# A fixed engine order for the query, key and value projections of a hybrid encoder layer

## The chip, the cores and the metric

One NeuronCore of a Trainium2 chip runs the whole layer in one launch. The metric is device time in microseconds, the median of the runs of the kernel. PE is the tensor engine (matrix products and transposes by product), DVE the vector engine, ACT the scalar engine, POOL the gpsimd engine, SP the queue from which this kernel issues its DMAs, also the transposing ones.

## The reference, cut to what matters

The layer normalizes x (1024 tokens by 1024), projects it to everything that its three branches need, and adds the gated branches' sum back to x. The part around the change makes queries, keys and values of eight heads from small latents:

```
q = (rmsnorm(q_lat, q_norm_g) @ w_uq).reshape(B, S, 8, 96)
kv = (rmsnorm(kv_lat, kv_norm_g) @ w_ukv).reshape(B, S, 8, 64 + 64)
k_nope, v = split_cols(kv, (64, 64))
k = concatenate([k_nope, k_rope], axis=-1)      # k_rope: 32 columns, the same for all heads
q = rope_tail(rmsnorm(q, q_head_g), cos, sin)
k = rope_tail(rmsnorm(k, k_head_g), cos, sin)
```

The gates (silu of 512 columns for each of two branches, sigmoids of 3 x 1024) are products of the normalized x with other columns of the same input weight. All is float32; each product is made as three, from the high and low parts of both sides.

## The kernel before, in words

Phase 1 normalizes x, turned with features in partitions (tiles hh and hl, high and low part), and makes the latents of eight blocks of 128 tokens. Then comes the loop of this case, one step for each block t:

- stD(t) (line 322) rotates the shared key columns (rope_k's four DVE operations, lines 327 to 330), makes the value product on PE (6 matmuls of 512 columns, line 333), which ACT and DVE read out as high and low part (line 335, through evac, lines 95 and 96) and SP stores; then the key product (6 matmuls, line 340), its squares on ACT (343), their sums on DVE (345), the power -1/2 on POOL (105) and the multiplications on DVE (348, 349); then the queries in two groups of four heads (9 matmuls of 384 columns each, line 359) with the same norm (362 to 367), and their rotation on POOL (370 to 374).
- stC(t + 1) (line 311) turns the next block's latents by PE into tile tr, and ACT and DVE read them out as high and low part (lath, latl).
- stE(t) (line 376) copies the 16-bit halves of keys and queries into pl (two DVE copies each, line 381), and SP issues two transposing DMAs each (line 382) into plt. Keys and queries share the one buffer of plt.
- stF(t - 1) (line 384) puts the turned halves together again on ACT (four reads of plt for keys, four for queries, line 391, into pw), scales them on ACT into the high part (line 98) and on DVE into the low part (line 99) of qkt, which SP stores (line 395). Each of keys and queries is done in two groups of four heads. An edge (issue_after) keeps it behind the last query square of step t.

PE is filled with dense products of the gate columns (class method feat, lines 518 to 535; tile fm while this loop runs, mm later): a generator yields one matmul of 512 columns at a time, and pull(n) asks for n of them. An item is 128 feature columns, 48 matmuls in two halves of 24. A half's result is read out by ACT (line 603) and DVE (604). The weights of the next item are split into high and low part on POOL (lines 74 and 80, tiles whi and wlo), in one piece where self.parts is 1, in quarters at the third, 11th, 19th and 27th matmul of the running item where it is 4; behind the last quarter SP is asked for the item after. The loop pulls 9 at five places of each step from t = 3 on, none for t = 0 to 2, and 60 behind the loop. What comes next, phase 2, goes on pulling from the same generator.

The order of the instructions on each engine is not the order of the code: a scheduler lays the queues out when the program is built, by priority in the order of the code and by when it expects an operand to be ready. manual_schedule(engines=...) keeps the order of the code on the engines it lists; phase 1 has it for PE (closed before this loop) and the attention stages later have it too. Engines wait for one another by semaphores that the framework sets.

PSUM has eight banks: in this loop tr takes two, the projections (mm) three, the dense products (fm) three. lath, latl, pw and qkt have two buffers each; plt, kn, qn, sq and vst have one.

Of the kernel before, what the change touches and what calls it, by code (L numbers as in the profile page):

```python
# [62 lines left out]
class K:  # L63
# [161 lines left out]
    def phase1(self, sr):  # L225
        tc, nc, a, d = self.tc, self.nc, self.a, self.d
        v, gp = nc.vector, nc.gpsimd
        with ExitStack() as st:
# [93 lines left out]
            def stD(tb, pulls):  # L322
                hi, lo = LT.pop(tb)
                _, kro, spe = HN.pop(tb)
# [6 lines left out]
                pv = ps.tile([P, 4, 2, DV], F32, name="mm", bufs=3)  # L331
                for k in range(2):
                    self.mm3(pv, hi[:, 3 + k, :], lo[:, 3 + k, :], wkh[:, k, 512:], wkl[:, k, 512:], k == 0, k == 1)
                vst = wd.tile([P, 4, 4, DV], F32R, name="vst")
                self.evac(pv, vst[:, :, 0:4:3, :], vst[:, :, 1:3, :])
                nc.sync.dma_start(d["v"][:, tb].rearrange("p h c -> p (h c)"), vst.rearrange("p a b c -> p (a b c)").bitcast(F32))
                self.pull(pulls)
                pk = ps.tile([P, H, DN], F32, name="mm", bufs=3)
                for k in range(2):
                    self.mm3(pk, hi[:, 3 + k, :], lo[:, 3 + k, :], wkh[:, k, :512], wkl[:, k, :512], k == 0, k == 1)  # L340
                kn = KN[tb] = wd.tile([P, H, DH], F32, name="kn")
# [4 lines left out]
                v.tensor_scalar_add(s[:, :H], s[:, :H], spe)  # L346
                self.rstd(s[:, H:], s[:, :H], DH)
                v.tensor_tensor(out=kn[:, :, :DN], in0=pk, in1=s[:, H:].unsqueeze(2).broadcast_to([P, H, DN]), op=ALU.mult)
                v.tensor_tensor(out=kn[:, :, DN:], in0=kro[:, 3, :].unsqueeze(1).broadcast_to([P, H, DR]),
                                 in1=s[:, H:].unsqueeze(2).broadcast_to([P, H, DR]), op=ALU.mult)  # L350
                self.pull(pulls)
                qn = QN[tb] = wd.tile([P, H, DH], F32, name="qn")
                s = wd.tile([P, 2 * H], F32, name="qst", bufs=2)
                pqs = []
                for g in range(2):
                    pq = ps.tile([P, 4, DH], F32, name="mm", bufs=3)
                    pqs.append(pq)
                    for k in range(3):
                        self.mm3(pq, hi[:, k, :], lo[:, k, :], wqh[:, k, g * 384:(g + 1) * 384], wql[:, k, g * 384:(g + 1) * 384], k == 0, k == 2)
                    hs = slice(4 * g, 4 * g + 4)  # L360
                    sq = wd.tile([P, H, DN], F32, name="sq").rearrange("p a b -> p (a b)")[:, :4 * DH].rearrange("p (a b) -> p a b", b=DH)
                    self.last = nc.scalar.activation(out=sq, in_=pq, func=AF.Square).ins
                    rs = slice(H + 4 * g, H + 4 * g + 4)
                    v.tensor_reduce(out=s[:, hs], in_=sq, axis=AX.X, op=ALU.add)
                    self.rstd(s[:, rs], s[:, hs], DH)
                    self.pull(pulls)
                    v.tensor_tensor(out=qn[:, hs, :], in0=pq, in1=s[:, rs].unsqueeze(2).broadcast_to([P, 4, DH]), op=ALU.mult)
# [8 lines left out]
            def stE(tb):  # L376
                for N, n in ((KN, "k"), (QN, "q")):
                    src, pl = N[tb], self.pl[n]
                    t = N[tb] = wd.tile([P, 2, H, P], U16, name="plt", bufs=1)
                    for x in range(2):  # L380
                        v.tensor_copy(pl[:, x, :, :DH], _halves(src, x))
                        nc.sync.dma_start_transpose(t[:, x], pl[:, x].rearrange("p a b -> p (a b)"))

            def stF(tb):
                ts = slice(tb * P, (tb + 1) * P)
                for src, dst, i in ((KN.pop(tb), d["k"], 1), (QN.pop(tb), d["q"], 0)):
                    for g in range(2):
                        hs = slice(4 * g, 4 * g + 4)
                        w = wd.tile([DH, 4, P], F32, name="pw", bufs=2)
                        for x in range(2):  # L390
                            nc.scalar.copy(_halves(w, x), src[:DH, x, hs])  # L391
                        t = wd.tile([DH, 4, 2, P], F32R, name="qkt", bufs=2)
                        self.evac(w, t[:, :, 0, :], t[:, :, 1, :], self.hg[:, i:i + 1])
                        for x in range(2):
                            nc.sync.dma_start(dst[4 * g:4 * g + 4, :, x, ts].rearrange("h d s -> d h s"), t[:, :, x, :].bitcast(F32))
# [64 lines left out]
            self.mm = lambda hf: ps.tile([P, 512], F32, name="fm", bufs=3)  # L460
# [4 lines left out]
            for t in range(TB):  # L465
                pulls = 9 if t > 2 else 0
                stD(t, pulls)
                if t + 1 < TB:
                    stC(t + 1)
                self.pull(pulls)  # L470
# [759 lines left out]
```

## Time and profile before

| | |
|---|---|
| median of 3 runs | 1171.45 us (1171.41 to 1172.24) |
| the profiled execution | 1175.43 us |
| its span, first to last instruction | 1173.3 us |
| mean granted TensorE clock | 0.986 |
| busy in the span: PE, DVE, POOL, ACT | 96%, 61%, 49%, 47% |
| matmuls | 5458 |

A profile is one execution, recorded by the chip. Times in it count from the start of the span. A matmul's duration in it is modelled and overlaps the next one's, so how fast PE works is read from the distance of starts. In the views, an arrow (kst <- sq) means that the first tile is made from the second; a wait names the waiting instruction first and what released it behind the arrow. The lines are those of the kernel before; a line can be that of a helper (evac, rstd, split), which several places call.

### The profile page before, as it was taken

How to read it: one execution, taken by the hardware profiler on the slowest of the kernel's cores; microseconds unless marked ns; L12 is line 12 of the kernel's file. 1: busy time of each engine (PE TensorE's matmuls, PEld its weight loads, DVE VectorE, ACT ScalarE, POOL GpSimd, SP SyncE). 2: the span in 40 equal slices, each digit the busy share in tenths (PEclk: the TensorE clock that was granted, in tenths of full speed). 3: DMA queues.
4: the chain of work that ended last, by engine and by line, in shares of the span. 5: the costliest groups of instructions: out<-in, count | busy, mean ns of one | idle time of the engine just before them, and what ended most of it. 6: DMA issues, size and time to landing. Idle time of an engine off the chain costs nothing.

```text
span 1173.3 us, 15384 instructions
## 1 busy us (share of the span) xinstructions
PE 1131.3 (96%) x5458; PEld 949.7 (81%) x5458; DVE 713.0 (61%) x1077; ACT 548.3 (47%) x821; POOL 576.7 (49%) x520
## 2 busy tenths in 40 slices
PE   7999899899999999998989999999999999999998
PEld 7998787778888888887868877878778878888887
DVE  6997686243335433454269999999999205655221
ACT  6446575511011114656358878878778312322100
POOL 4455475243324553345655777776785823333200
PEclk8999999999999999999989999999999989999999
DMA  8427999923232333455889989999997597545341
GB/s 300 150 94 185 240 232 238 261 101 107 73 124 73 126 108 81 90 144 158 243 209 208 220 215 213 211 229 236 213 198 167 162 408 291 160 140 169 105 148 50
DMA packets 284717, 207.75 MB, mean 177 GB/s; under 512 B 201664, under 2 KB 253504, under 8 KB 284544
## 3 DMA queue, kind: packets, MB, share of 16 engines
q1 hardware_dynamic: 284640, 206.76, 65.7%
q8 instruction: 43, 0.70, 0.2%
q14 instruction: 34, 0.28, 0.1%
HBM read 108.14 MB, written 50.33 MB: 135 GB/s over the span
## 4 chain that ended last, share of the span: by engine, by line
PE 27%; DVE 14%; DMA 6%; issue 4%; POOL 2%; ACT 1%; SPq 0%; ACTq 0%; DVEq 0%; POOLq 0%
DVE pl L85 6%; DVE mx L989 4%; PE mm L714 4%; PE mm L716 4%; PE mm L712 4%; DMA plt<-pl 3%; DVE ptl L1014 3%; PE mm L111 2%; PE mm L109 2%; PE mm L110 2%; PE mm L527 2%; PE mm L529 2%; PE mm L531 2%; PE po L1028 1%; PE s L984 1%
## 5 line engine op out<-in xcount | busy, mean ns | idle before, releaser
L527 PE MATMUL mm<-hh,whi 128*128 128x512 f32 x672 | 265.0, 394 | 3.5 <-DVE sg L604 3.5
L529 PE MATMUL mm<-hl,whi 128*128 128x512 f32 x672 | 264.4, 393 | 0.0
L531 PE MATMUL mm<-hh,wlo 128*128 128x512 f32 x672 | 262.9, 393 | 1.2 <-POOL wlo L80 1.2
L74 POOL TENSOR_SCALAR whi<-wraw 128x256 fp32r<-128x256 f32 (+1 forms) x128 | 117.2, 916 | 201.1 <-PE pm L761 76.4
L90 ACT COPY pw<-plt 128x1024 uint16<-128x1024 uint16 (+1 forms) x160 | 197.8, 1302 | 6.8 <-DMA plt<-pl 6.5
L80 POOL TENSOR_TENSOR wlo<-wraw,whi 128x256 fp32r<-128x256 f32 (+1 forms) x129 | 178.4, 1383 | 11.2 <-ACT whi L76 1.4
L527 PEld LDWEIGHTS mm<-hh,whi 128*128 128x128 f32 x672 | 127.5, 190 | 30.5 <-DVE sg L604 4.3
L531 PEld LDWEIGHTS mm<-hh,wlo 128*128 128x128 f32 x672 | 127.5, 190 | 28.3 <-POOL wlo L80 1.6
L529 PEld LDWEIGHTS mm<-hl,whi 128*128 128x128 f32 x672 | 127.6, 190 | 26.0
L85 DVE COPY pl<-p 128x1024 uint16<-128x1024 uint16 x144 | 127.7, 927 | 17.1 <-DMA plt<-pl 9.3
L1010 POOL TENSOR_SCALAR pth<-pw 128x1024 fp32r<-128x1024 f32 x64 | 78.6, 1228 | 91.5 <-ACT pw L90 87.7
L984 PE MATMUL s<-k,q 96*128 96x512 f32 x384 | 101.1, 399 | 6.1 <-ACT p L992 5.9
L1014 DVE TENSOR_TENSOR ptl<-pw,pth 128x1024 fp32r<-128x1024 f32 x64 | 98.8, 1543 | 6.8 <-POOL pth L1010 6.4
L992 ACT ACTIVATE p<-s,mx 128x1024 f32<-128x1024 f32 x64 | 71.5, 1117 | 60.9 <-DVE mx L989 60.2
L984 PEld LDWEIGHTS s<-k,q 96*128 96x128 f32 x384 | 72.2, 190 | 25.7 <-ACT p L992 9.6
L989 DVE TENSOR_REDUCE mx<-s 128x1 f32<-128x1024 f32 x64 | 77.2, 1206 | 5.8 <-PE s L984 5.4
L689 ACT ACTIVATE sg<-sg 128x1024 f32<-128x1024 f32 x24 | 25.5, 1061 | 92.6 <-DMA sg<-d_r 92.6
L391 ACT COPY pw<-plt 96x512 uint16<-96x512 uint16 x64 | 43.8, 771 | 27.1 <-DMA plt<-plq 20.9
L621 ACT ACTIVATE sg<-mm,small 128x512 f32<-128x512 f32 x48 | 32.7, 683 | 46.5 <-PE mm L531 34.2
L719 DVE TENSOR_TENSOR acc<-mm,sg 128x512 f32<-128x512 f32 x16 | 10.9, 689 | 53.0 <-PE mm L716 42.6
L76 ACT CAST whi<-wraw 128x1024 fp32r<-128x1024 f32 x9 | 9.5, 1051 | 68.1 <-PE mm L529 66.8
L1028 PE MATMUL po<-pth,v 128*128 128x256 f32 x256 | 38.4, 293 | 0.0
(323 smaller groups left out, 2331.3 us busy)
## 6 DMA issues: line engine op xcount, KB each, us to landing
wraw<-in_w_feat SPq DMA_DIRECT2D x48, 512.0 KB, 4.1
d_r<-sg SPq DMA_DIRECT2D x24, 512.0 KB, 3.4
sg<-d_r SPq DMA_DIRECT2D x24, 512.0 KB, 4.2
d_k<-qkt SPq DMA_DIRECT2D x32, 192.0 KB, 3.0
d_q<-qkt SPq DMA_DIRECT2D x32, 192.0 KB, 2.9
q<-d_q SPq DMA_DIRECT2D x32, 192.0 KB, 3.6
wraw<-in_w_br SPq DMA_DIRECT2D x12, 512.0 KB, 4.2
k<-d_k SPq DMA_DIRECT2D x14, 384.0 KB, 5.1
```

What stands on the lines that cost most here:

```text
L74: nc.gpsimd.tensor_scalar(out=hi, in0=raw, scalar1=1.0, scalar2=1.0, op0=ALU.mult, op1=ALU.mult)
L80: e.tensor_tensor(out=lo, in0=raw, in1=hi.bitcast(F32), op=ALU.subtract)
L85: self.nc.vector.tensor_copy(pl[:, x], _halves(src, x))
L90: self.nc.scalar.copy(_halves(out, x), plt[:, x])
L527: mm(o, w1, self.hh[:, k, c], start=k == 0, stop=False)
L529: mm(o, w1, self.hl[:, k, c], start=False, stop=False)
L531: mm(o, w2, self.hh[:, k, c], start=False, stop=k == KT - 1)
L984: nc.tensor.matmul(s[:, c], q[:, qi, ts], k[:, ki, c], start=s_, stop=e_)
L989: v.reduce_max(out=mx[:, 1:2], in_=s, axis=AX.X, negate=True)
L992: nc.scalar.activation(out=p, in_=s, func=AF.Exp, bias=mx[:, 1:2], accum_out=mx[:, 2:3])
L1010: nc.gpsimd.tensor_scalar(out=parts(i)[0], in0=p, scalar1=1.0, scalar2=1.0, op0=ALU.mult, op1=ALU.mult)
L1014: v.tensor_tensor(out=lo, in0=PW.pop(i), in1=hi.bitcast(F32), op=ALU.subtract)
```

## The change

The functions stD, stE and stF are taken apart into values, rope_k, keys, keys2, queries, queries2, rope_q, turn and parts, with the same operations. The loop calls them in a fixed order under manual_schedule for PE, DVE, ACT and POOL; SP's queue is still laid out by the scheduler. The projections get four banks instead of three, the dense products two instead of three. The pulls are 9 at five places for steps 3 to 7, as before, 30 in a ninth step and 30 behind the loop. The splits of the weights go in quarters inside the loop.

```
-                pv = ps.tile([P, 4, 2, DV], F32, name="mm", bufs=3)
+            mm_ps = lambda sh: ps.tile(sh, F32, name="mm", bufs=4)
...
-            def stE(tb):
-                for N, n in ((KN, "k"), (QN, "q")):
-                    src, pl = N[tb], self.pl[n]
-                    t = N[tb] = wd.tile([P, 2, H, P], U16, name="plt", bufs=1)
+            def turn(tb, N, n):
+                src, pl = N[tb], self.pl[n]
+                t = N[tb] = wd.tile([P, 2, H, P], U16, name="plt", bufs=1)
+                for x in range(2):
+                    v.tensor_copy(pl[:, x, :, :DH], _halves(src, x))
+                    nc.sync.dma_start_transpose(t[:, x], pl[:, x].rearrange("p a b -> p (a b)"))
+
+            def parts(tb, N, n, i):
+                ts = slice(tb * P, (tb + 1) * P)
+                src, dst = N.pop(tb), d[n]
+                for g in range(2):
+                    hs = slice(4 * g, 4 * g + 4)
+                    w = wd.tile([DH, 4, P], F32, name="pw", bufs=2)
                     for x in range(2):
...
+                        nc.scalar.copy(_halves(w, x), src[:DH, x, hs])
+                    t = wd.tile([DH, 4, 2, P], F32R, name="qkt", bufs=2)
+                    self.evac(w, t[:, :, 0, :], t[:, :, 1, :], self.hg[:, i:i + 1])
+                    for x in range(2):
+                        nc.sync.dma_start(dst[4 * g:4 * g + 4, :, x, ts].rearrange("h d s -> d h s"), t[:, :, x, :].bitcast(F32))
...
-            self.mm = lambda hf: ps.tile([P, 512], F32, name="fm", bufs=3)
+            self.mm = lambda hf: ps.tile([P, 512], F32, name="fm", bufs=2)
...
-            for t in range(TB):
-                pulls = 9 if t > 2 else 0
-                stD(t, pulls)
-                if t + 1 < TB:
-                    stC(t + 1)
-                self.pull(pulls)
-                stE(t)
+            E = mybir.EngineType
+            man = st.enter_context(ExitStack())
+            man.enter_context(tc.manual_schedule(engines={E.PE, E.DVE, E.Activation, E.Pool}))
+            self.parts = 4
+            for t in range(TB + 1):
+                n = 9 if 2 < t < TB else 0
+                if t < TB:
+                    rope_k(t)
+                    values(t)
+                    self.pull(n)
+                    if t + 1 < TB:
+                        stC(t + 1)
                 if t:
-                    with tc.issue_after(self.last):
-                        stF(t - 1)
-            stF(TB - 1)
-            self.pull(60)
+                    parts(t - 1, KN, "k", 1)
+                    turn(t - 1, QN, "q")
+                if t < TB:
+                    keys(t)
+                    self.pull(n)
+                    queries(t, 0)
+                    keys2(t)
+                    self.pull(n)
+                    queries(t, 1)
+                    queries2(t, 0)
+                    self.pull(n)
+                else:
+                    self.pull(30)
+                if t:
+                    parts(t - 1, QN, "q", 0)
+                if t < TB:
+                    turn(t, KN, "k")
+                    queries2(t, 1)
+                    rope_q(t)
+                    self.pull(n)
+            man.close()
+            self.parts = 1
+            self.pull(30)
```

keys ends with the power of the norm and keys2 multiplies by it; queries and queries2 share the work of a group in the same way.

## Rows read from the trace of the kernel before

**Rows 1.** The page's first part: busy us, share of the span, instructions.

```profile
PE 1131.3 (96%) x5458; PEld 949.7 (81%) x5458; DVE 713.0 (61%) x1077; ACT 548.3 (47%) x821; POOL 576.7 (49%) x520
```

**Rows 2.** Stretches: length, busy PE, PEld, DVE, ACT, POOL, granted clock, DMA, GB/s.

```profile
74.20:116.20 42.00, 41.92 (x209) 35.91 (x208) 33.31 (x81) 24.31 (x49) 27.80 (x25) 1.00 0.68 174
116.20:201.20 85.00, 78.43 (x357) 65.59 (x357) 62.95 (x116) 56.08 (x97) 47.16 (x43) 0.98 1.00 240
```

**Rows 3.** Waits from 76 to 206 us: total us, times, longest us.

```profile
ACT pw L391 <- DMA plt<-plq: 19.0, 7, 5.5
...
DVE vst L96 <- ACT vst L95: 9.6, 4, 4.5
...
PE mm L109 <- DVE vst L96: 6.6, 4, 2.3
```

**Rows 4.** Timeline of SP's queue, transposes alone: start, us, instruction.

```profile
88.79 2.72 SPq L382 DMA_TRANSPOSE plt<-plk  x2
...
100.35 2.61 SPq L382 DMA_TRANSPOSE plt<-plq  x2
...
107.03 4.96 SPq L382 DMA_TRANSPOSE plt<-plk  x2
...
157.86 4.34 SPq L382 DMA_TRANSPOSE plt<-plk  x2
...
208.10 2.62 SPq L382 DMA_TRANSPOSE plt<-plk  x2
```

**Rows 5.** Timeline of ACT around one handover.

```profile
150.60 1.33 ACT L98 ACTIVATE qkt<-pw,small 96x512 fp32r<-96x512 f32 x2
...
155.80 2.03 ACT L391 COPY pw<-plt 96x512 uint16<-96x512 uint16 x3
```

**Rows 6.** Groups by form, 74 to 201.2 us: busy us, mean ns, idle before.

```profile
L527 PE MATMUL fm<-hh,whi 128*128 128x512 f32 x96 | 38.1, 397 | 0.0
...
L99 DVE SCALAR_TENSOR_TENSOR qkt<-pw,small,qkt 96x512 fp32r<-96x512 f32 x25 | 20.8, 839 | 7.0 <-ACT qkt L98 7.0
...
L381 DVE COPY plk<-kn 128x768 uint16<-128x768 uint16 x16 | 10.8, 714 | 0.0
```

**Rows 7.** Timeline of PE; in brackets the idle time before and its releaser.

```profile
111.83 0.39 PE L527 MATMUL fm<-hh,whi 128*128 128x512 f32 x1
...
115.00 0.39 PE L531 MATMUL fm<-hh,wlo 128*128 128x512 f32 x1
...
191.57 0.45 PE L109 MATMUL mm<-wuqh,lath 128*128 128x384 f32 x1 [2.27 <-DVE vst L96]
...
200.98 0.39 PE L531 MATMUL fm<-hh,wlo 128*128 128x512 f32 x1
...
209.30 0.73 PE L527 MATMUL mm<-hh,whi 128*128 128x512 f32 x1 [2.49 <-DVE sg L604]
```

**Rows 8.** The first stretch, instructions on fm alone: busy PE, PEld, DVE, ACT.

```profile
74.20:116.20 42.00, 23.30 (x92) 16.93 (x92) 1.35 (x2) 1.67 (x3) 1.00 0.68 174
```

**Rows 9.** POOL: one query rotation, then quarters of a split, 560 to 800 us.

```profile
90.17 0.47 POOL L370 TENSOR_TENSOR sq<-qn,tabs 128x128 f32<-128x128 f32 x1 [1.37 <-DVE qn L367]
...
91.96 0.74 POOL L374 TENSOR_TENSOR qn<-qn,sq 128x256 f32<-128x256 f32 x1
...
L80 POOL TENSOR_TENSOR wlo<-wraw,whi 128x256 fp32r<-128x256 f32 x44 | 42.0, 955 | 3.5
L74 POOL TENSOR_SCALAR whi<-wraw 128x256 fp32r<-128x256 f32 x44 | 38.2, 869 | 10.3 <-DMA wraw<-in_w_feat 9.0 <-PE mm L529 1.2
```

**Rows 10.** Timeline of DVE in step 0.

```profile
85.55 2.28 DVE L349 TENSOR_TENSOR kn<-kro,kst 128x256 f32<-128x256 f32 x1
```

**Rows 11.** Stretches behind two of PE's waits, columns as in rows 2.

```profile
192.00:195.00 3.00, 3.00 (x12) 2.80 (x11) 2.48 (x6) 1.12 (x2) 0.00 (x0) 0.56 1.10 213
195.00:198.00 3.00, 3.00 (x13) 2.43 (x12) 1.93 (x6) 2.27 (x5) 2.49 (x2) 0.88 1.01 259
...
209.00:212.00 3.00, 2.70 (x7) 2.15 (x8) 2.51 (x5) 1.36 (x3) 0.00 (x0) 0.57 0.95 180
```

More of the change, by code (lines that the diff above doesn't have):

```diff
@@ L320, in stC, with values, rope_k @@
                 LT[tb] = (hi, lo)
-            def stD(tb, pulls):
-                hi, lo = LT.pop(tb)
-                _, kro, spe = HN.pop(tb)
+            mm_ps = lambda sh: ps.tile(sh, F32, name="mm", bufs=4)
+            KS, QS = {}, {}
+            def values(tb):
+                hi, lo = LT[tb]
+                pv = mm_ps([P, 4, 2, DV])
+                for k in range(2):
+                    self.mm3(pv, hi[:, 3 + k, :], lo[:, 3 + k, :], wkh[:, k, 512:], wkl[:, k, 512:], k == 0, k == 1)
+                vst = wd.tile([P, 4, 4, DV], F32R, name="vst")
+                self.evac(pv, vst[:, :, 0:4:3, :], vst[:, :, 1:3, :])
+                nc.sync.dma_start(d["v"][:, tb].rearrange("p h c -> p (h c)"), vst.rearrange("p a b c -> p (a b c)").bitcast(F32))
+            def rope_k(tb):
+                kro = HN[tb][1]
                 kp = kro[:, 0, :]
@@ L330, in stD, with keys @@
                 v.tensor_tensor(out=kro[:, 3, :], in0=kro[:, 1, :], in1=kro[:, 2, :], op=ALU.add)
-                pv = ps.tile([P, 4, 2, DV], F32, name="mm", bufs=3)
[L332 to L336, printed above, removed]
-                self.pull(pulls)
-                pk = ps.tile([P, H, DN], F32, name="mm", bufs=3)
+            def keys(tb):
+                hi, lo = LT[tb]
+                pk = mm_ps([P, H, DN])
                 for k in range(2):
                     self.mm3(pk, hi[:, 3 + k, :], lo[:, 3 + k, :], wkh[:, k, :512], wkl[:, k, :512], k == 0, k == 1)
-                kn = KN[tb] = wd.tile([P, H, DH], F32, name="kn")
                 sq = wd.tile([P, H, DN], F32, name="sq")
@@ L345, in stD, with keys2 @@
                 v.tensor_reduce(out=s[:, :H], in_=sq, axis=AX.X, op=ALU.add)
-                v.tensor_scalar_add(s[:, :H], s[:, :H], spe)
+                v.tensor_scalar_add(s[:, :H], s[:, :H], HN[tb][2])
                 self.rstd(s[:, H:], s[:, :H], DH)
+                KS[tb] = (pk, s)
+            def keys2(tb):
+                pk, s = KS.pop(tb)
+                kro = HN.pop(tb)[1]
+                kn = KN[tb] = wd.tile([P, H, DH], F32, name="kn")
                 v.tensor_tensor(out=kn[:, :, :DN], in0=pk, in1=s[:, H:].unsqueeze(2).broadcast_to([P, H, DN]), op=ALU.mult)
@@ L350, in stD @@
                                  in1=s[:, H:].unsqueeze(2).broadcast_to([P, H, DR]), op=ALU.mult)
[L351 to L367, printed above, removed]
@@ new lines, in queries @@
+            def queries(tb, g):
+                hi, lo = LT[tb]
+                if g == 0:
+                    QS[tb] = [wd.tile([P, 2 * H], F32, name="qst", bufs=2)]
+                s = QS[tb][0]
+                pq = mm_ps([P, 4, DH])
+                QS[tb].append(pq)
+                for k in range(3):
+                    self.mm3(pq, hi[:, k, :], lo[:, k, :], wqh[:, k, g * 384:(g + 1) * 384], wql[:, k, g * 384:(g + 1) * 384], k == 0, k == 2)
+                hs, rs = slice(4 * g, 4 * g + 4), slice(H + 4 * g, H + 4 * g + 4)
+                sq = wd.tile([P, H, DN], F32, name="sq").rearrange("p a b -> p (a b)")[:, :4 * DH].rearrange("p (a b) -> p a b", b=DH)
+                nc.scalar.activation(out=sq, in_=pq, func=AF.Square)
+                v.tensor_reduce(out=s[:, hs], in_=sq, axis=AX.X, op=ALU.add)
+                self.rstd(s[:, rs], s[:, hs], DH)
@@ L368, in stD, with queries2, rope_q @@
+            def queries2(tb, g):
+                s, pq = QS[tb][0], QS[tb][1 + g]
+                hs, rs = slice(4 * g, 4 * g + 4), slice(H + 4 * g, H + 4 * g + 4)
+                if g == 0:
+                    QN[tb] = wd.tile([P, H, DH], F32, name="qn")
+                v.tensor_tensor(out=QN[tb][:, hs, :], in0=pq, in1=s[:, rs].unsqueeze(2).broadcast_to([P, 4, DH]), op=ALU.mult)
+            def rope_q(tb):
+                qn = QN[tb]
                 rb = wd.tile([P, H, DN], F32, name="sq")[:, :, :DR]
@@ L384, in stF @@
[L384 to L395, printed above, removed]
+            def turn(tb, N, n):
[4 more added lines that the diff above has]
+                    nc.sync.dma_start_transpose(t[:, x], pl[:, x].rearrange("p a b -> p (a b)"))
```

3 lines of the change are left out of this document (removed).

## The prediction, made before the changed kernel was run

> **What bounds the kernel now.** I read the page's first part, then the stretches of the stage that the diff touches, then its waits, then the transposes on SP's queue. The page says that PE is busy 96% of the span [rows 1], so any gain or loss here is PE time. The stage runs from about 74.3 us to 201.2, its last dense product starting at 200.98 [rows 7]. By stretches, PE is busy there almost throughout, while DVE, ACT and POOL are each busy 55 to 80% [rows 2]. PE's waits in it are four, 6.6 us together, all of a projection matmul (L109) for DVE's read of the value product (L96) [rows 3]. DVE in turn waited for ACT's copy of it, and ACT's largest wait, 19.0 us, is for the transposes of the queries [rows 3].
>
> That last wait shows the stage's second limit. Keys and queries share one buffer, plt, so the transposes go strictly in turn: keys, ACT reads plt four times (L391), queries, four reads, keys again. The four reads before the keys of one step end at 155.80 + 2.03 = 157.83, and the next pair starts at 157.86 [rows 4, 5]. I call one such turn a handover. The first pair of queries starts at 100.35 and the eighth pair of keys at 208.10, thirteen handovers later [rows 4]: 107.75 / 13 = 8.29 us each, 16.6 per step. The fastest took 107.03 - 100.35 = 6.68. PE's own work: 126.9 us less 6.6 of waits and 1.7 of half clock (below) is 118.6; the 288 dense products (3 x 96 [rows 6]) at (115.00 - 111.83) / 14 = 0.227 [rows 7] are 65.4 of it, so the projections and turns of one step are 53.2 / 8 = 6.7. PE stays busy over a chain of 16.6 us per step because 92 of the dense products run before 116.2, during steps 0 to 2 [rows 8], though the loop pulls none for these steps: the order was free.
>
> **The change, part by part.**
>
> Four banks for projections. The value product's bank no longer holds up the next projection: at most 6.6 us of waits go, and 1.7 of half clock behind the last one (0.56 for 3 us and 0.88 for 3 us, which is 1.3 + 0.4 [rows 11]).
>
> Two banks for dense products. A half takes 24 x 0.227 = 5.4 us, its reading by ACT and DVE some 1.5 (estimated as L98 and L99, 0.72 and 0.75). If ACT stands at a transpose when a half ends, the next half but one waits. I put the cost at nothing as long as PE waits for the chain anyway, which is what follows; without that cover it is ACT's wait, 5.5 us at its longest [rows 3].
>
> Splits in quarters. Four times (0.87 + 0.96) [rows 9] is 7.3 us of POOL per item; POOL is busy 75 of 127 us [rows 2]. Hidden, but each quarter now stands behind the reciprocal roots and the query rotation of its step.
>
> The fixed order on ACT and DVE, the part that matters. In a handover ACT now does read, read, scale (L98), read, read, scale, DVE the low part (L99) after each, and only then DVE's copy (L381) whose end lets SP issue the next pair. Before, the copy was done early and the pair started with the end of the fourth read. Added between fourth read and next pair: the first scale now stands among the reads, 1.33 - 0.72 = 0.61; the second after them, 0.63 + 0.72 instead of 0.77, 0.58 [rows 5]; the low part, some 0.75, and one copy, some 0.55 (0.84 and 0.71 on average with the collisions of now [rows 6]); three passings on of some 0.03. Sum 2.6. The rest of the order (key norm and first query norm in one half, second query norm, rotation of the keys, value and latent reads in the other) is 3 to 6 us of DVE, less than a landing and the reads behind it, so I put it at nothing; if transposes landed 2 us sooner, it would take their place. The edge that held the scaling of the step before behind the last query square (issue_after) goes into the fixed order. SP is not in the list, so its queue stays free; two stores (L395) that are ready half a microsecond before the copies may go first and cost up to 0.6. On the other side, the pairs are 2.6 to 5.0 us long to issue [rows 4] and are long where DMA's share is 1.00 rather than 0.68 [rows 2]; the same bytes now take longer, so I take off 0.5, a choice. A handover: 8.29 + 2.6 - 0.5 = 10.4. Ends: 6.68 + 2.6 = 9.3, and 8.9 + 2.6 = 11.5 (8.9 being 8.29 and the 0.6 of the stores).
>
> The fixed order on PE. Steps 0 to 2 pull nothing and nothing may be moved up: the 92 products of rows 8 come after. In step 8 there are 30 pulls and behind the loop 30 more.
>
> The sum for the end of the stage. The first pair of keys starts at 88.79 now [rows 4], behind a key multiplication of 2.28 us [rows 10] that stood beside a full-width split on POOL; without that, and with a fixed order, some 86. Fourteen handovers to the eighth pair of keys: 86 + 14 x 10.4 = 231.6. After it DVE copies the second half and norms the second queries (1.0); POOL rotates them, 91.96 + 0.74 - 90.17 = 2.5 [rows 9]; behind that stands the last quarter of the sixth item's weights, which is pulled at the end of step 7 (the 219th of 225 pulls), 1.8 [rows 9]. Only then can PE run this item's 48 products, 10.9, and having stood idle it should run its beginning at half clock, 1.7 as above. Together 17.9: the dense products end at 249.5 instead of 201.2, **+48.3**.
>
> Behind the stage. Now PE waits 2.49 us before 209.30 for a feature product's reading, which ACT did late, behind reads of a late transpose, and then runs at 0.57 for 3 us [rows 7, 11], some 1.7 with what follows. With the chain nearly done when PE gets there I take this as gone: **-4.2**; bounds 0 and -6.
>
> Total +44. The profiled execution took 1175.43 us, its span 1173.3 and 2.1 around it; it lies 4.0 above the median of the runs, 1171.45, and I add to the median: **1215.5**. All later stages are PE's, so nothing catches up.
>
> The Trainium skill (Perfetto Trace Analysis, Identifying the Most-Contended Engine) says that the engine of highest occupancy is to be optimized first and its gaps closed. By that rule the change is right, since PE is at 96% and its gaps here are bank waits; the sum by it would be that of the third rival.
>
> **The rivals.**
>
> Handovers not longer. If landings come so much sooner with less traffic that a handover stays at 8.29: 86 + 116.1 + 17.9 = 220.0, +18.8 - 4.2, **1186**. For it: the fastest handover of now is 6.68, from a stretch with little traffic. Against: 2.6 us of added work by rows.
>
> Worse chain. ACT and DVE wait in order for PE as well (a feature product's reading stands ahead of the reads), and SP's queue may be laid out badly. At 11.5 a handover and nothing regained: 264.9, +63.7, **1235**, or more.
>
> PE alone decides, which ends faster. The mechanism: bank waits. If a handover stayed off the path, the 6.6 us, both half clocks (3.4) and the 2.49 would go: 1171.45 - 12.5 = **1159**. It decides from the point where two handovers fit under PE's work in a loaded step, 6.7 + 45 x 0.227 = 16.9, so 8.4 each, and where also steps 1 and 2, with 6.7 us of PE work, take no more than now. Against: steps 1 and 2 have two handovers each, 13.4 at their fastest. The occupancy rule named above speaks for it; the traces bear it out little, since the longest wait of rows 3 is ACT's, not PE's.
>
> The order does not bind (the scheduler still moves products up): about no change, 1165 to 1174.
>
> **How the numbers follow.** Forecast (1200 to 1235) 0.66; handovers not longer (1180 to 1200) 0.20; beyond 1235 0.05; PE alone 0.06; no change 0.03. The likeliest gives 1215.5. Its own range has the handover's ends: 9.3 gives 234.1, +28.7, 1200; 11.5 gives 1235. To hold 8 in 10 I take in the first rival: 1185 to 1235. No change is within 0.2%, 2.3 us, about what a measurement of this kernel can tell. Faster 0.06, same 0.03, slower 0.91.
>
> **What would show it.** Right: pairs of transposes 9.3 to 11.5 us apart, starting behind L99 and L381; ACT's wait for plt far above 19 us; PE with gaps of several us in every step, the granted clock near 0.5 behind them, and no fm products before some 107 us (the projections' banks let PE run about one step ahead of the chain: 86 + 20.8); a last wait of fm for POOL's wlo, its end near 250. Later stages unchanged. Wrong: handovers at 8.3 or less, or fm ending near 200 with PE busy throughout.

## The result, and the profile after

The changed kernel takes 1209.11 us (median of 4 runs, 1205.71 to 1213.7), the kernel before 1171.43 in the same session: a ratio of **1.0328 [1.0307, 1.0349]**, 37.7 us slower. The forecast was 1215.5 us, in a range of 1185 to 1235. In all that follows, line numbers are those of the kernel that was run.

The page's first part (busy us, share, instructions) shows the same work in a longer span: PE's share falls from 96% to 94% [rows 1].

```profile
PE 1138.0 (94%) x5458; PEld 953.8 (79%) x5458; DVE 709.9 (59%) x1077; ACT 553.9 (46%) x821; POOL 585.1 (49%) x556
```

The stretches of the stage come next, columns as in rows 2, and a third stretch that did not belong to the stage before:

```profile
74.20:116.20 42.00, 28.73 (x136) 24.13 (x134) 24.98 (x61) 22.07 (x42) 16.38 (x18) 0.88 0.61 160
116.20:201.20 85.00, 73.56 (x322) 61.00 (x323) 56.57 (x123) 52.02 (x85) 46.73 (x58) 0.93 0.80 197
201.20:243.90 42.70, 31.86 (x119) 25.33 (x117) 20.70 (x39) 22.35 (x35) 24.16 (x33) 0.82 0.81 197
...
96.00:107.00 11.00, 5.57 (x15) 4.75 (x15) 7.70 (x17) 6.97 (x13) 3.63 (x3) 0.55 0.65 146
```

PE was busy 41.9 of the first 42 us; now it is busy 28.7. All engines are busy less in the first two stretches, and DMA's share falls too: nothing is overloaded, everything waits. The last line takes in an idle stretch of PE and what ran behind it: the granted clock is 0.55 there, near the lower of its two levels.

Where PE stood, from its timeline (first and last product of the stage, and its longest idle times with their releasers):

```profile
101.43 0.80 PE L109 MATMUL mm<-wkh,lath 128*128 128x512 f32 x1 [8.62 <-DVE kn L360]
...
110.85 0.40 PE L570 MATMUL fm<-hh,whi 128*128 128x512 f32 x1
...
120.58 0.79 PE L109 MATMUL mm<-wkh,lath 128*128 128x512 f32 x1 [6.92 <-DVE kn L360]
...
236.53 0.79 PE L570 MATMUL fm<-hh,whi 128*128 128x512 f32 x1 [3.64 <-DVE sg L647]
...
243.67 0.39 PE L574 MATMUL fm<-hh,wlo 128*128 128x512 f32 x1
```

The first dense product runs at 110.85, and the last at 243.67 instead of 200.98 [rows 7]: 42.7 us later. The waits from 76 to 245 us (total, times, longest), to be held against rows 3:

```profile
DVE qkt L99 <- ACT qkt L98: 54.9, 27, 6.0
...
ACT pw L410 <- DMA plt<-plk: 37.6, 15, 5.8
...
PE mm L109 <- DVE kn L360: 18.2, 4, 8.6
PE fm L570 <- DVE sg L647: 13.2, 4, 5.9
...
ACT pw L410 <- DMA plt<-plq: 11.5, 11, 5.6
```

PE's waits for the value product's reading are gone, as four banks promise. In their place stand 18.2 us for the bank of the keys (L360) and 13.2 us of dense products for the reading of a half (L647). ACT's two waits for plt together are 49.1 us, "far above 19" as forecast.

SP's transposes and, below them, ACT and DVE in one handover:

```profile
87.90 2.71 SPq L401 DMA_TRANSPOSE plt<-plk  x2
...
126.04 2.63 SPq L401 DMA_TRANSPOSE plt<-plk  x2
135.47 2.66 SPq L401 DMA_TRANSPOSE plt<-plq  x2
...
225.09 3.06 SPq L401 DMA_TRANSPOSE plt<-plk  x2
```

```profile
129.59 0.78 ACT L410 COPY pw<-plt 96x512 uint16<-96x512 uint16 x1 [3.71 <-DMA plt<-plk]
...
131.41 0.72 ACT L98 ACTIVATE qkt<-pw,small 96x512 fp32r<-96x512 f32 x1
132.04 1.39 ACT L410 COPY pw<-plt 96x512 uint16<-96x512 uint16 x2
133.47 0.72 ACT L98 ACTIVATE qkt<-pw,small 96x512 fp32r<-96x512 f32 x1
```

```profile
134.22 0.75 DVE L99 SCALAR_TENSOR_TENSOR qkt<-pw,small,qkt 96x512 fp32r<-96x512 f32 x1 [1.30 <-ACT qkt L98]
134.89 1.02 DVE L400 COPY plq<-qn 128x768 uint16<-128x768 uint16 x2
```

The fourth read ends at 132.04 + 1.39 = 133.43, but the next pair leaves at 135.47, behind the scaling (L98), the low part (L99) and the first copy (L400): 2.04 us in which the buffer lies free. Before, the pair left at once [rows 4, 5]. From the first pair of keys to the eighth, (225.09 - 87.90) / 14 = **9.80 us** a handover. The 8.29 of before was counted from the first pair of queries, over thirteen. Counted so, the changed kernel has (225.09 - 97.43) / 13 = 9.82; counted from the first pair of keys, the kernel before has (208.10 - 88.79) / 14 = 8.52 [rows 4].

Close behind the stage 7.3 of the 42.7 us come back, at three waits of PE in the kernel before that the changed kernel does not have: 4.4 at the one before 209.30 and its half clock [rows 7, 11], 1.3 and 1.6 at two of 0.96 and 1.17 us before 233.93 and 241.45. From there on the dense products are 35.0 to 36.4 us late: no later stage takes part. The two profiled executions differ by 3.4 us less than 35.4 (1207.41 - 1175.43 = 32.0), because the profiled execution of the kernel before lost about that much near 950 us; its windows show PE at half clock there, where the changed kernel's show 1.00:

```profile
952.00:956.00 4.00, 4.00 (x11) 3.02 (x11) 0.69 (x1) 1.26 (x2) 0.00 (x0) 0.50 1.02 419
```

### The profile page after: what moved, and what is told of

Its sections match the earlier page's. It is cut to its first block, busy times and chain, and to the rows that moved or that the text cites. A ratio compares the mean times of both kernels' runs of the same rounds, so it can differ in the third digit from the quotient of the medians.

```text
span 1205.6 us, 15407 instructions
## 1 busy us (share of the span) xinstructions
PE 1138.0 (94%) x5458; PEld 953.8 (79%) x5458; DVE 709.9 (59%) x1077; ACT 553.9 (46%) x821; POOL 585.1 (49%) x556
## 4 chain that ended last, share of the span: by engine, by line
PE 28%; DVE 12%; DMA 5%; issue 3%; POOL 3%; ACT 2%; SPq 0%; ACTq 0%; POOLq 0%; DVEq 0%
DVE pl L85 5%; PE mm L757 4%; PE mm L759 4%; PE mm L755 4%; DVE mx L1032 3%; DMA plt<-pl 3%; DVE ptl L1057 2%; PE mm L111 2%; PE mm L110 2%; PE mm L109 2%; PE mm L570 2%; PE mm L572 2%; PE mm L574 2%; PE s L1027 2%; PE po L1071 1%
## 5 line engine op out<-in xcount | busy, mean ns | idle before, releaser
L74 POOL TENSOR_SCALAR whi<-wraw 128x256 fp32r<-128x256 f32 (+1 forms) x146 | 123.7, 848 | 207.9 <-PE pm L804 76.3
L80 POOL TENSOR_TENSOR wlo<-wraw,whi 128x256 fp32r<-128x256 f32 (+1 forms) x147 | 183.0, 1246 | 13.7 <-ACT whi L76 2.1
L1027 PEld LDWEIGHTS s<-k,q 96*128 96x128 f32 x384 | 72.0, 190 | 26.7 <-ACT p L1035 10.8
L410 ACT COPY pw<-plt 96x512 uint16<-96x512 uint16 x64 | 46.7, 764 | 49.3 <-DMA plt<-plk 37.6
L99 DVE SCALAR_TENSOR_TENSOR qkt<-pw,small,qkt 96x512 fp32r<-96x512 f32 x32 | 24.6, 770 | 54.9 <-ACT qkt L98 54.9
L570 PE MATMUL fm<-hh,whi 128*128 128x512 f32 x96 | 40.9, 426 | 14.3 <-DVE sg L647 13.2
```

The lines of the kernel that those rows point to most:

```text
L74: nc.gpsimd.tensor_scalar(out=hi, in0=raw, scalar1=1.0, scalar2=1.0, op0=ALU.mult, op1=ALU.mult)
L80: e.tensor_tensor(out=lo, in0=raw, in1=hi.bitcast(F32), op=ALU.subtract)
L570: mm(o, w1, self.hh[:, k, c], start=k == 0, stop=False)
L1027: nc.tensor.matmul(s[:, c], q[:, qi, ts], k[:, ki, c], start=s_, stop=e_)
```

## The experiments

Theory: the fixed order lengthens the handover (scaling, low part and copy between the last read and the next pair), and the chain of handovers sets the stage's end. Rivals: the two banks for dense products; the place of the products in PE's order; the single buffer as such; the splits in quarters. Ratios are to the kernel before in the same session (1169.4 to 1171.5 us).

| kernel | us | ratio |
|---|---|---|
| changed kernel | 1209.11 | 1.0328 [1.0307, 1.0349] |
| free order | 1192.47 | 1.0184 [1.0169, 1.0199] |
| copies first | 1203.2 | 1.0275 [1.0255, 1.0294] |
| even fill | 1206.84 | 1.0298 [1.0279, 1.0317] |
| two plt buffers | 1203.02 | 1.0275 [1.0258, 1.0292] |
| banks 3 and 3 | 1200.41 | 1.0265 [1.0246, 1.0284] |
| copies first, stores behind | 1187.02 | 1.0146 [1.0126, 1.0165] |
| free order, banks 3 and 3 | 1178.87 | 1.0078 [1.0064, 1.0093] |
| the same, splits whole | 1181.03 | 1.0099 [1.0083, 1.0115] |
| copies, stores, banks | 1183.42 | 1.0115 [1.0094, 1.0136] |
| the same, even fill | 1185.23 | 1.0119 [1.0101, 1.0138] |
| the same, gaps filled | 1168.96 | 0.998 [0.9966, 0.9993] |
| kernel before, two plt buffers | 1174.63 | 1.0039 [1.0025, 1.0052] |

**Free order.** The changed kernel without its fixed order.

```diff
-            man.enter_context(tc.manual_schedule(engines={E.PE, E.DVE, E.Activation, E.Pool}))
```

> The changed kernel without its fixed order: the scheduler lays out all queues again; banks (four and two), quarter splits and the pulls of the changed kernel stay. Order theory (the copies stand behind the scaling in the handover of plt, and nothing fills steps 0 to 2): pairs of transposes about 8.3 us apart instead of 9.8, some 90 dense products before step 3, the dense products end at 195 to 206 us, time 1160 to 1178. Bank theory (two banks for dense products and quarters on POOL cost it): the 13 us of PE waits for DVE L647 and more stay, time 1190 or above.

1192.47: the order alone is worth 16.6 us of the 37.7, not all. A handover does not fall to the 8.3 us expected; it takes (223.46 - 89.12) / 14 = 9.60, the two transposes of most pairs lying apart. Yet the loop's last dense product runs at 208.58, 7.6 us late instead of 42.7: with the order free, PE's products wait far less for the chain. They keep up with the kernel before for the first half of the stage (the 97th runs 0.7 us earlier), then fall behind, most of it in one wait of PE behind the loop (the 361st product):

```profile
238.49 0.80 PE L569 MATMUL mm<-hh,whi 128*128 128x512 f32 x1 [13.21 <-DVE sg L646]
```

It waits for a dense half that was done at 214.41 to be read. On ACT that reading stands behind reads of plt; the timeline of ACT shows it begun right at their end:

```profile
235.88 1.38 ACT L410 COPY pw<-plt 96x512 uint16<-96x512 uint16 x2 [1.97 <-DMA plt<-plq]
237.13 0.58 ACT L645 ACTIVATE sg<-mm 128x512 f32<-128x512 f32 x1
```

So there is a second loss, a half that stands unread. The tile of these products (mm, behind the loop) has three banks in every version; whether the loop's two banks put the reading so late, or only the way in which the scheduler laid out ACT's queue, this run does not tell.

**Copies first.** The copies of a tensor ahead of the scaling of the other, the transposes still behind the reads.

```diff
                 for x in range(2):
-                    v.tensor_copy(pl[:, x, :, :DH], _halves(src, x))
                     nc.sync.dma_start_transpose(t[:, x], ...)
+            def copies(tb, N, n):
+                for x in range(2):
+                    v.tensor_copy(self.pl[n][:, x, :, :DH], _halves(N[tb], x))
...
+                    copies(t - 1, QN, "q")
                     parts(t - 1, KN, "k", 1)
...
+                if t < TB:
+                    copies(t, KN, "k")
                 if t:
                     parts(t - 1, QN, "q", 0)
```

> The changed kernel, fixed order, with DVE's two copies of each turn moved ahead of the scaling of the other tensor; the transposes still wait for the four reads of plt. Order theory: the second scale's part beyond the reads (0.58), the low part (0.75), a copy (0.55) and two passings leave the handover, 9.8 becomes 7.8, fourteen of them are 28 us, steps 0 to 2 stay unfilled: time 1176 to 1190. Bank theory: no more than 5 us, 1204 or above. Buffer theory (plt itself binds): the handover falls as well, so this run does not tell it from the order theory; the run with two buffers does.

A miss: a handover stayed at (223.81 - 86.52) / 14 = 9.81 us. SP's queue, which the fixed order does not cover, shows why:

```profile
172.40 1.10 SPq L417 DMA_DIRECT2D d_k<-qkt  x2
173.68 1.28 SPq L400 DMA_TRANSPOSE plt<-plq  x1
175.06 1.56 SPq L417 DMA_DIRECT2D d_k<-qkt  x2
176.67 1.56 SPq L400 DMA_TRANSPOSE plt<-plq  x1
```

Two stores of the second half of the heads, which wait for DVE's low part, are laid between the two transposes. The pair is split by the very wait that the copies had been moved past. This was a reading of the trace until the stores were moved (below).

**Even fill.** 7 products in each fill of all eight steps instead of 9 from the fourth on, 3 and 2 behind instead of 30 and 30.

```diff
-                n = 9 if 2 < t < TB else 0
+                n = 7 if t < TB else 0
...
-                    self.pull(30)
+                    self.pull(3)
...
-            self.pull(30)
+            self.pull(2)
```

> The changed kernel with its 285 pulls spread evenly: 7 at the five places of every step, 3 in the ninth and 2 behind the loop, instead of 9 from step 3 on, 30 and 30. Order theory: handovers stay at 9.7 to 9.9 us since the chain does not depend on PE; PE has its dense products behind it when the chain ends, so they end near 231 instead of 244, and some of the 13 us is given back behind the stage: 1194 to 1202. If handovers alone made the time, with no part for the place of the products: 1206 to 1212. Bank theory: waits for DVE L647 grow, time not below 1205.

1206.84, a miss: within the interval of no gain. The first dense products now stand ahead of the first keys, whose pair leaves at 97.46 instead of 87.90. A handover takes (239.89 - 97.46) / 14 = 10.17. What PE gained early the chain lost.

**Two plt buffers.** plt with two buffers, and one staging tile pl for keys and queries, to make room.

```diff
-                t = N[tb] = wd.tile([P, 2, H, P], U16, name="plt", bufs=1)
+                t = N[tb] = wd.tile([P, 2, H, P], U16, name="plt", bufs=2)
...
-            self.pl = {n: wd.tile([P, 2, H, P], U16, name="pl" + n) for n in "kq"}
+            pl = wd.tile([P, 2, H, P], U16, name="pl")
+            self.pl = {"k": pl, "q": pl}
```

> The changed kernel with two buffers for plt (and, for the room, one for pl, which keys and queries then share). Order theory: the pair is issued behind DVE's copy, which stands behind the scaling anyway, so handovers stay at 9.6 to 10.0 us and the time at 1204 to 1214. Buffer theory (the shared plt is what makes the handover): pairs no longer alternate with the reads, 8 us or less apart, time 1185 or below.

1203.02, a little under the expected 1204 to 1214; a handover still takes (222.88 - 86.38) / 14 = 9.75 us. So the single plt alone does not make the cadence of the fixed order; it is no clean proof, since the shared staging tile also holds a copy back until the pair before it has been read.

**Banks 3 and 3.** Three banks for projections and three for dense products; the order kept.

```diff
-            mm_ps = lambda sh: ps.tile(sh, F32, name="mm", bufs=4)
+            mm_ps = lambda sh: ps.tile(sh, F32, name="mm", bufs=3)
...
-            self.mm = lambda hf: ps.tile([P, 512], F32, name="fm", bufs=2)
+            self.mm = lambda hf: ps.tile([P, 512], F32, name="fm", bufs=3)
```

> The changed kernel with three banks for projections and three for feature products instead of four and two; the order is kept. If the two banks cost what the waits of the feature products for the reading of a half show (13.2 us, of which 4 stand behind the last keys and 6 in one place before them), the time falls to 1196-1204 and those waits of PE are gone. If the chain of handovers alone sets the end, PE's waits only move to the projections: 1205-1213, and the handover stays at 9.8.

1200.41, as the bank theory had it; the 13.2 us of waits for L647 are gone, though a handover is no shorter, (225.84 - 87.20) / 14 = 9.90. PE's waits for the keys' bank grew from 18.2 to 26.7 us in all, the longest of them early in the stage (this one, and 9.51 us before 120.67). Even so the loop's last dense product runs 8.0 us earlier, at 235.65, for the chain ran on as before:

```profile
101.46 0.77 PE L109 MATMUL mm<-wkh,lath 128*128 128x512 f32 x1 [7.79 <-DVE kn L360]
```

**Copies first, stores behind.** The run with the copies first, and the stores of a tensor issued behind the transposes of the other.

```diff
                     for x in range(2):
-                        nc.sync.dma_start(dst[...], t[:, :, x, :].bitcast(F32))
+                        st_.append((dst[...], t[:, :, x, :].bitcast(F32)))
...
-                    parts(t - 1, KN, "k", 1)
+                    st_ = parts(t - 1, KN, "k", 1)
                     turn(t - 1, QN, "q")
+                    stores(st_)
...
                     turn(t, KN, "k")
+                if t:
+                    stores(st_)
```

> The changed kernel with VectorE's copies of a tensor ahead of the scaling of the other, and with the stores of the scaled parts issued behind the two transposes, so that SP passes nothing between the last reading and the pair. If SP's stores between the transposes gave back the gain of the copies, the pair leaves when the last reading is done: the handover falls from 9.8 to 7.6-8.3 us and the time to 1175-1190. If something else makes the cadence (the landing of the stores, the two qkt buffers, the order on ScalarE), the handover stays above 9.3 and the time above 1198.

1187.02: this shows both the handover and SP's part in it. The pair leaves the moment ACT has read (SP's timeline, then ACT's):

```profile
87.35 2.73 SPq L400 DMA_TRANSPOSE plt<-plk  x2
...
95.04 2.62 SPq L400 DMA_TRANSPOSE plt<-plq  x2
...
101.13 0.30 SPq L422 DMA_DIRECT2D d_q<-qkt  x1
102.42 2.63 SPq L400 DMA_TRANSPOSE plt<-plk  x2
...
124.78 3.40 SPq L400 DMA_TRANSPOSE plt<-plq  x2
...
206.89 2.63 SPq L400 DMA_TRANSPOSE plt<-plk  x2
```

```profile
101.00 1.38 ACT L413 COPY pw<-plt 96x512 uint16<-96x512 uint16 x2
```

The first five handovers, from 87.35 to 124.78, take 7.49 us each. The first five of the changed kernel took (135.47 - 87.90) / 5 = 9.51, which is 2.03 more, and in the one read above 2.04 us of scaling, low part and copy stood between. Over the stage the mean is (206.89 - 87.35) / 14 = 8.54; the last nine take 9.12, with dense products and their weights beside them, pairs of up to 5.29 us on SP, and DMA's share at 0.92.

**Free order with banks 3 and 3**, and **with whole splits as well.** Both edits as above; for the second, the line that asks for quarters is left away.

```diff
-            self.parts = 4
```

> The order left to the scheduler, as in the run with a free order (1192.5), and three banks for each. If the bank split makes the rest of the loss that the free order left (21 us), the time comes back to 1168-1177 and the 13-us wait of a feature product for the reading of a half is gone. If the quarters or the new sequence of the code make it, it stays at 1186-1196.

> Free order, three banks for each, and weight splits whole: the resources of the kernel before, only the sequence of the code is the new one. 1166-1177 if banks or quarters made the rest of the loss; if the sequence itself does (the readings of a turn and the transposes laid elsewhere on the queues), 1184-1196, within 4 us of the run that has the quarters.

1178.87 and 1181.03. The exchange of banks gives back 1.0184 - 1.0078, which is 12.4 us, though not the whole 21; the quarters cost nothing that shows. The 13.21 us wait is gone: ACT reads that half at 225.53 instead of 237.13, and PE waits 5.62 us for a reading before 217.98, where the kernel before waits 2.49 [rows 7]. Since the tile behind the loop has three banks either way, it is not shown how much of this is the banks and how much a queue laid out anew. What is left, 1.0078 to 1.0099, belongs to what still differs, the new sequence of the code (with its ninth step and without the edge), by which the scheduler lays out the queues: in both runs most pairs of transposes lie apart, 2 to 5 us from the first to the second.

**Copies, stores and banks together.**

> Copies first and stores behind the transposes (1187.0 by itself) together with three banks for each (1200.4 by itself, 8.7 below the changed kernel). If handovers and banks are two separate losses, the gains add: 1174-1182. If both runs took away the same waits at the end of the stage, little is added: 1184-1188.

1183.42, between the two expectations. By the ratios, the parts took 1.82% and 0.63% off, both together 2.13%: half of the banks' gain adds. Where the other half went is not shown; with a bank less for the projections, the first dense product runs at 117.91 instead of 107.64. 14 us were left over the kernel before. PE's timeline shows what they are:

```profile
85.22 0.77 PE L109 MATMUL mm<-wkh,lath 128*128 128x512 f32 x1 [2.44 <-DVE kn L360]
...
100.46 0.76 PE L109 MATMUL mm<-wkh,lath 128*128 128x512 f32 x1 [6.96 <-DVE kn L360]
...
115.22 0.76 PE L109 MATMUL mm<-wkh,lath 128*128 128x512 f32 x1 [5.61 <-DVE kn L360]
```

```profile
74.20:116.20 42.00, 26.09 (x114) 22.20 (x113) 28.79 (x71) 25.61 (x48) 19.35 (x21) 0.79 0.71 182
116.20:201.20 85.00, 83.00 (x378) 70.15 (x377) 61.67 (x127) 57.17 (x92) 49.42 (x65) 0.96 0.87 210
```

From 116.2 us PE is busy 83 of 85 us, as it never was in the changed kernel; up to there it stands idle for 16 us, behind the queries of each of the first three steps, and no product may be moved into the gap. Now PE's late start sets the end, not the chain: the eighth pair of keys leaves at 209.51, 1.4 us later than in the kernel before, and the last dense product runs at 219.03, 18.1 us later.

**The same with an even fill.** The fills of the even fill above.

> The run before this one with 7 feature products in each fill of all eight steps, 3 and 2 behind (285 as before), in place of 9 from the fourth step on. With shorter handovers TensorE's own work at the end of the stage may set its end; then the products that move into the first three steps take 6-12 us off it: 1165-1175. If the chain still sets it, the fill changes as little as it did with the long handovers (2 us): 1174-1181.

1185.23, no change, and outside both expectations. The chain starts late again: the first pair of keys leaves at 98.12 instead of 87.04, for the fill in step 0 stands ahead of the keys, and its first product waits in order for its weights:

```profile
79.74 0.63 PE L585 MATMUL fm<-hh,whi 128*128 128x512 f32 x1 [3.29 <-ACT whi L76]
```

**The same with the gaps filled.** Instead of the even fill: one fill at the end of each of the first three steps, as large as PE's gap there, and none behind the eighth.

```diff
                     rope_q(t)
-                    self.pull(n)
+                    self.pull(n or (9, 28, 24)[t])
...
-                    self.pull(30)
+                    self.pull(0)
...
-            self.pull(30)
+            self.pull(0)
```

> Copies first, stores behind and three banks for each (1183.4), with the 61 products from behind the eighth step put into the idle stretches that TensorE showed behind the queries of the first three steps (9, 28 and 24 of them, one fill at the end of each step). If what is left over the kernel before (14 us) is TensorE's late start on the products, 1168-1177, first pair of keys still near 87, and the wait of TensorE for the second step's bank (2.8, 7.3 and 5.9 us of idle time) filled. If products put in early hold up the chain, as with the even fill (first pair 98), 1179-1188.

1168.96, ratio 0.998 [0.9966, 0.9993] with 12 runs against 17: the loss is gone, and 0.2% more, little beyond the interval. The chain starts early (SP's timeline), PE's three waits have shrunk to 0.26, 1.63 and 0.57 us, and the clock stays up:

```profile
86.15 2.73 SPq L400 DMA_TRANSPOSE plt<-plk  x2
...
205.19 2.62 SPq L400 DMA_TRANSPOSE plt<-plk  x2
```

```profile
84.24 0.50 PE L109 MATMUL mm<-wkh,lath 128*128 128x512 f32 x1 [0.26 <-DVE kn L360]
99.00 0.47 PE L109 MATMUL mm<-wkh,lath 128*128 128x512 f32 x1 [1.63 <-DVE kn L360]
...
198.90 0.39 PE L589 MATMUL fm<-hh,wlo 128*128 128x512 f32 x1
```

```profile
74.20:116.20 42.00, 36.38 (x174) 30.01 (x173) 31.91 (x68) 27.91 (x51) 25.49 (x29) 1.00 0.73 188
116.20:201.20 85.00, 84.90 (x401) 71.94 (x400) 68.65 (x135) 57.06 (x94) 53.02 (x71) 1.00 1.00 239
```

The last product of the stage starts at 198.90, 2.1 us before that of the kernel before [rows 7], with PE busy 84.9 of the last 85 us.

**The kernel before with two plt buffers.** The edit of the run with two buffers, in the kernel before.

> The kernel before with two buffers for the turned tensor and one shared staging tile. If the handover through the single buffer bounds the stage in the kernel before (13 of 8.29 us), the pairs leave earlier, TensorE's waits for the banks shrink and the time falls to 1158-1167. If the readings on ScalarE and VectorE bound it, or the stage's end is TensorE's own work, it stays at 1167-1174.

1174.63, a little slower, outside both expectations. It is no clean test: the shared staging tile and the two qkt buffers bring waits of their own (waits from 76 to 245 us):

```profile
ACT qkt L98 <- DMA d_k<-qkt: 13.5, 12, 3.7
...
DVE pl L381 <- DMA plt<-pl: 7.0, 6, 2.7
```

The first of these two was 2.9 us in the kernel before. In the profiled execution the stage ends 0.8 us later than there, and right behind it two waits of dense products for DVE's reading (4.05 us before 211.63, where the kernel before has 2.49, and 1.17 before 225.43) bring that to 3.6 of the 4.6 us. A handover, (205.74 - 88.67) / 14 = 8.36, was hardly shorter than 8.52, so the run does not tell what a shorter one would be worth.

## Why the prediction was right, step by step

**The handover: right, a little too long.** The forecast was 10.4 us (9.3 to 11.5), 9.80 was measured. The added work was priced well: 132.04 - 131.41 = 0.63 for the first scaling among the reads and 2.04 behind the last read, 2.7 in all where the sum had 2.6, and the run with copies first and stores behind took 2.03 of the 2.04 away again in its first five. Too small was the 0.5, called a choice, that was taken off for thinner traffic: counted alike, 8.29 + 2.67 - 9.82 = 1.14. The issue of the pairs makes 0.96 of that; over these thirteen turns it took 3.75 us on average before and 2.78 now. The reason given, DMA's share, does not fit: the pair at 97.43 left in 2.64 us with the share at 1.02. The last section has what goes with long pairs, and the kernel before had one of 5.69 us, beyond the 2.6 to 5.0 that the prediction read. Over fourteen handovers the 0.6 make 8.4 us, the largest error of the sum.

**SP's queue: the right suspect, in another place.** The stores ahead of the pair were given up to 0.6 us. In the changed kernel they cost nothing, because the copies came later still. As soon as the copies were moved up, the stores took back the whole gain.

**The first pair and the eighth.** 86 and 231.6 were forecast; 87.90 and 225.09 came, the second early by the handover's error.

**The tail behind the eighth pair: the length right, the cause wrong.** 17.9 us were forecast, 243.9 - 225.09 = 18.8 came. But the last long wait is not for POOL's last quarter (1.26 us before 231.69); it is for DVE's reading of a dense half, which the fixed order puts behind the last handover's scaling and copies. That the length came out is luck.

**Two banks for dense products: the step that failed.** "I put the cost at nothing as long as PE waits for the chain anyway." PE does so for most of the stage, but not at its end: two of its three long waits for a reading, 5.93 us before 217.40 and 3.64 before 236.53, come with the chain's last links, when PE has nothing else to do. A third bank for dense products, taken from the projections, gave 0.63% (7.4 us) in the fixed order; in the free one the same exchange gave 1.06% (12.4 us), there through a reading that was laid out earlier. That alternative was named at 5.5 us, ACT's longest wait, and then dropped; it belonged in the sum, where it would have taken the place of the wait for POOL.

**Four banks for projections.** Right that L96's waits would go, and that the sum took no gain from it: PE waits 18.2 us for the keys' bank instead. The Trainium skill (Perfetto Trace Analysis, Optimization Strategy) says that a gap which repeats on the engine that should be saturated can mean too few buffers. The traces agree that these gaps are waits for a bank: with one bank less they were 26.7 us in all instead of 18.2. But closing them was not what the time hung on, for that kernel, with its third bank for dense products, was 0.63% faster.

**Quarters hidden.** Right as far as was tried: whole splits, in free order, were no faster.

**PE's order and clock.** Right: no dense product before 110.85 (forecast 107), gaps of up to 8.6 us, the granted clock at 0.54 to 0.57 behind the long ones.

**Behind the stage.** 4.2 us were to come back, at most 6. At the wait that was named 4.4 did, and 2.9 more at the two waits further on that the prediction did not look at. Together the trace has +35.4 instead of +44: handovers 8.4 less and regain 3.1 more, first pair and tail 1.9 and 0.9 longer. The median of the runs rose by 37.7.

**The rivals.** Handovers did get longer, so 1186 fell; they stayed under 11.5 and time was regained, so 1235 did. PE alone (1159) fell too, as a forecast for this change. The Trainium skill (Perfetto Trace Analysis, Identifying the Most-Contended Engine and Optimization Strategy) would have the busiest engine's gaps closed first. The change closed the bank waits of 6.6 us that such a reading finds, and PE then stood idle for longer than before on work of engines that are busy half the time. In the last version, with PE busy 84.9 of 85 us, the rule and the trace agree on what the time is made of; they part on which edit closes a gap.

**What the sum did not see.** The prediction took the kernel before as two limits side by side, PE's work and the handovers, and gave the whole loss to the handovers; it named the empty first three steps, but gave them no term. Counted alike over fourteen, a handover takes 8.52 us in the kernel before, 8.54 in the run with stores behind and (205.19 - 86.15) / 14 = 8.50 in the version with the gaps filled. The run with stores behind has its eighth pair of keys at 206.89, 1.2 us before the kernel before, and still its last dense product runs 21.7 us later, at 222.68. In the free order it is the other way round: long handovers of 9.60, and a last dense product only 7.6 us late. So the handovers alone do not set when the dense products end; what counts is how far the order lets PE run ahead of them. In the kernel before and in the version with the gaps filled, the loop's last product starts before the eighth pair leaves (200.98 and 208.10, 198.90 and 205.19).

That makes the 37.7 us three losses in one stage, under the fixed order: the longer handover, dense halves that wait to be read, and PE's empty first three steps. They overlap, as the combined runs show: the first two give 2.13% together where 1.82% and 0.63% were measured alone, and with the third, 1.35% more, the whole of it and a little over. The third alone was not measured, since the even fill delayed the first pair of keys.

Left open: why the last nine handovers of the run with stores behind take 9.12 us where the first five take 7.49 (the longer pairs are only part of it), and how much of the free order's remaining 0.8% is the split pairs; no run laid them together with the order left free.

## What to carry to other kernels

A fixed order freezes idle time as well as work: for every place where an engine will wait in order, put filling work there, as much as the wait is long, and none ahead of the first link of a chain that others wait for. Where one buffer is handed from one tensor to the next, let nothing stand between the last read and the next write but the write itself, and look at the queue that issues it too: here stores between two transposes took back the whole gain of moving the copies away. A bank or a buffer that costs nothing while something else is late has to be priced again at the stage's end, where nothing else is late.

## What the runs showed of the hardware

A pair of these transposes takes 2.6 us to issue on SP at its shortest, and up to 5.69 in the kernel before (5.29 in the run with stores behind). What goes with a long issue is a transfer issued before it on the same queue that has not landed. In the kernel before, the last of these is one of 512 KB at each long pair (a weight load wraw, a gate store d_gm or d_ga, or the values' store d_v), and nine of the ten pairs of over 3 us end within 0.4 us of its landing. The load of the first line here lands at 137.69, and the pair's issue ends at 137.50:

```profile
130.54 1.18 SPq L487 DMA_DIRECT2D wraw<-in_w_feat  x1
131.81 5.69 SPq L382 DMA_TRANSPOSE plt<-plq  x2
...
142.43 2.62 SPq L382 DMA_TRANSPOSE plt<-plk  x2
```

The other six pairs, with every earlier transfer landed or landing within 1.7 us, take 2.6 to 2.7. In the changed kernel fifteen pairs start with at most stores of 192 KB under way, which land within 2.8 us, and take 2.6 to 3.1; the one whose stores land 3.9 us after its start takes 3.78. DMA's share does not tell them apart: it is 1.02 over the changed kernel's pair at 97.43 (2.64 us) and 1.03 over the one at 131.81 above. No run moved these transfers alone, so this is a reading of the traces and not shown by experiment.

PE's idle time cost twice: in the changed kernel the granted clock fell to 0.54 to 0.57 behind each long gap, and in the stretch up to 116.2 us it was 0.88 (0.79 with copies, stores and banks together), against 1.00 once the gaps were filled.
